# A two-layer diffusion backbone: the later modulation vectors formed by VectorE alone

## The chip, the cores and the metric

The kernel runs on one NeuronCore of a Trainium2 chip. The metric is the device time of one execution in microseconds (us), the median of several runs. The engines are named as the profile names them: PE is TensorE (matmuls; PEld is its weight load), DVE is VectorE, ACT is ScalarE, POOL is GpSimd, SP is the engine whose queue issues the DMAs.

## The reference, cut to what matters

Two layers (`DEPTH = 2`) work on 256 latent tokens and 256 context tokens of width 1024. Each layer is a half feed-forward, a token mixer of four branches, and another half feed-forward. Each of these three is modulated by shift, scale and gate vectors that come from one large product per layer:

```python
for l in range(DEPTH):
    mod_x = jax.nn.silu(c) @ w_mod[l] + b_mod[l]        # 1024 -> 9 * 1024
    mod_c = (jax.nn.silu(c_ctx) @ w_mod[l] + b_mod[l])[None, :]
    ...
    x, xc = layer(x, xc, mod_x, mod_c, p, ctx_out)

def half_ffn(t, m, i):
    j = 6 * i
    hh = adaln(t, g[2 * i], m[j], m[j + 1])             # rms_norm(t, g) * (1 + scale) + shift
    return t + 0.5 * m[j + 2] * swiglu(hh, p['ffn_w_gate'][i], p['ffn_w_up'][i], p['ffn_w_down'][i])
```

So `w_mod` (two layers of 1024 x 9216) is multiplied by only two vectors, SiLU(c_ctx) and SiLU(c). Everything is float32.

## The kernel before, in words

Activations lie with features on partitions, `x[0..7]`, each 128 x 512 (256 context columns, then 256 latent ones). A weight tile of up to 128 x 2048 comes by one DMA into one of three `w` buffers. ACT copies it to a rounded high part `wh` (L150) and DVE subtracts to get the low part `wl` (L151), in halves; there are four buffers each of `wh` and `wl`, that is two tiles. `mm3` (L191 to L193) forms every product out of three matmuls: high by high, high by low, low by high. `ffn` runs, for each half of the hidden width, eleven gate-and-up tiles (`gu`: 2 x 8 products, 48 matmuls into the PSUM tiles A and B; `act` then multiplies on DVE at L455 and splits at L196 and L197) and eight down tiles (`dn`: 11 products, 33 matmuls, and the residual at L422). `plan` writes the order of the weight stream.

The 9216 modulation columns of a layer are 18 sets `s` of four blocks of 128. The first four sets of layer 0 are made at the start on PE (`mod_set`). The other 32 are made in the background of feed-forwards: `plan` puts 64 `mod` tiles (32 sets, two halves `h` of the input width) between the `gu` and `dn` tiles, 28 of them in the first feed-forward of layer 0, 12 in its second, 24 in the first of layer 1. `mod_bg` handles a tile. The tile has 128 input features on partitions and four blocks `k` of 512 modulation columns; for each block and for each of the two vectors `v`, DVE multiplies the block with the vector's 128 values (a scalar for each partition) and adds it to a running sum, L254 for the first and L256 for the others, 8 instructions a tile. This leaves two 128 x 512 partial sums in `ya` buffers. When two sets are ready, eight matmuls with a one-hot column matrix `sel` (L265, into PSUM D) add the 128 partitions up. After one or two such pairs ACT copies D out (L269), four transposes (L272, into C) put the features on partitions, and L277 adds the bias. `derive` makes the scale and gate constants of it.

The order on each engine is settled when the program is built, by a list scheduler that works from its own costs and from free buffers. Each engine then runs its row of instructions strictly in that order, waiting where a row's inputs or buffers aren't ready. The neighbourhood branch's bias tables are fetched (`nr`, small strided DMAs) and masked (`nb`) by `na_bias`, both pairs of heads at once at the branch's start.

Of the kernel before, what the change touches and what calls it, by code (L numbers as in the profile page):

```python
# [15 lines left out]
L = 2  # L16
D = 1024
# [12 lines left out]
O_G, O_BM, O_BG, O_CA, O_LW, O_LB, O_BA, O_BX, O_LAM = 0, 24, 96, 128, 134, 142, 144, 148, 152  # L30
# [5 lines left out]
class Net:  # L36
# [16 lines left out]
    BUFS = dict(b=12, nb=4, nr=4, ya=4, yp=4, m=8, a=6, l=5, r=3, t=2)  # L53
# [52 lines left out]
    def start_stream(self):  # L106
        self.q = self.plan()
        self.raw, self.split = {}, {}
        self.at_raw = self.at_split = self.at = 0
        tags = ["b"] * 12 + ["ya"] * 4 + ["yp"] * 4 + ["a"] * 4 + ["b"] * 8  # L110
        self.first = {}
        for s in range(4):
            if s == 1:
                self.fetch()
                self.fetch()
            for k in range(KC):
                t = self.blk(tags.pop(0))
                self.nc.sync.dma_start(t, self.a["mod"][0, s, k // 4][:, 512 * (k % 4):512 * (k % 4) + 512])
                self.first[s, k] = t
# [79 lines left out]
    def consts(self):  # L199
        nc = self.nc  # L200
# [9 lines left out]
        self.sv = self.sc[:, :, 0:2]  # L210
        self.sel = self.cp.tile([128, 2, 32], F32, name="sel")
# [14 lines left out]
        for c in range(KC):  # L226
# [3 lines left out]
                     (self.rep[0], self.a["rep"][0]), (self.rep[1], self.a["rep"][1])]  # L230
        self.part, self.group = {}, {}
# [12 lines left out]
    def mod_bg(self, l, s, h):  # L244
        nc = self.nc
        w = self.take("mod", l, s, h)[:].rearrange("p (k n) -> p k n", k=4)
        if h == 0:
            self.part[s] = [self.blk("ya"), self.blk("ya")]
        for k in range(4):
            for v in range(2):  # L250
                acc = self.part[s][v]
                sv = self.sv[:, 4 * h + k, v:v + 1]
                if h == 0 and k == 0:
                    nc.vector.tensor_scalar(acc, w[:, k], sv, None, op0=ALU.mult)  # L254
                else:
                    nc.vector.scalar_tensor_tensor(acc, w[:, k], sv, acc, op0=ALU.mult, op1=ALU.add)  # L256
        r = s % 6
        if h == 1 and r % 2 == 1:
            j = (r % 4) // 2
            last = r in (3, 5)  # L260
            if r in (1, 5):
                self.group = self.ps("D")
            g = self.group
            for q in range(4):
                nc.tensor.matmul(g[32 * q:32 * q + 32, :], self.sel[:, j], self.part[s - 1 + q // 2][q % 2],  # L265
                                 start=(r in (1, 5)), stop=last, tile_position=(0, 32 * q))
            if last:
                sb = self.blk("t")
                nc.scalar.activation(sb, g, AF.Copy)  # L269
                pt = self.ps("C", (128, 4, 128))  # L270
                for b in range(4):
                    nc.tensor.transpose(pt[:, b], sb[:, 128 * b:128 * b + 128], self.ident)  # L272
                v = pt[:].rearrange("p b (g v n) -> p g b v n", g=2, v=2)
                for jj in range(2 if r == 3 else 1):
                    s0 = s - 3 + 2 * jj if r == 3 else s - 1
                    bm = self.par[l][:, O_BM + 4 * s0:O_BM + 4 * s0 + 8].rearrange("p (g b) -> p g b", g=2)
                    nc.vector.tensor_tensor(self.mods[l][:, s0:s0 + 2], v[:, :, :, :, jj],  # L277
                                            bm.unsqueeze(3).to_broadcast([128, 2, 4, 2]), op=ALU.add)
                    self.derive(l, s0)
                    self.derive(l, s0 + 1)  # L280
# [276 lines left out]
    def na_bias(self, l, pr):  # L557
        nc = self.nc
        src = self.a["nb"]
        nb = []  # L560
        for h in (2 * pr, 2 * pr + 1):
            raw = self.blk("nr", (128, 2, 4, 64))
            for qb in range(2):
                for r in range(2):
                    o = src.offset + (l * 4 + h) * 465 + (7 - (2 * qb + r)) * 31 - 48
                    ap = bass.AP(tensor=src.tensor, offset=o, ap=[[1, 64], [31, 4], [1, 64]])
                    nc.sync.dma_start(raw[64 * r:64 * r + 64, qb], ap)
            t = self.blk("nb", (128, 2, 4, 64))
# [100 lines left out]
    def attend(self, step, segs, out, keys, queries, value, biases, sink):  # L669
# [7 lines left out]
        def scores(u):  # L677
# [8 lines left out]
            P[u] = self.softmax(S, nk(u), (lambda hh: bias[pr](hh, qb)) if sg else None, lambda hh: sink(pr, hh))  # L686

# [15 lines left out]
        for pr in range(2):  # L703
            bias[pr] = biases(pr)
# [59 lines left out]
    def mixer(self, l, H, nxt):  # L764
# [160 lines left out]
    def run(self):  # L925
# [45 lines left out]
def layout(x, c, ctx, c_ctx, w_mod, b_mod, norm_g, ffn_w_gate, ffn_w_up, ffn_w_down, w_in, b_gate, conv_a_w,  # L971
# [13 lines left out]
    A["mod"] = wm.transpose(0, 4, 1, 3, 2, 5, 6).reshape(L, 18, 2, 128, 2048)  # L985
# [57 lines left out]
```

## Time and profile before

| | us |
|---|---|
| median of 3 runs (2058.46 to 2063.48) | 2061.11 |
| the profiled execution's own time | 2066.55 |
| its span, first to last instruction | 2064.8 |
| PE busy | 2037.9 (99%) |
| DVE busy | 1311.4 (64%) |
| ACT busy | 805.3 (39%) |

Busy is the time in which an engine has at least one instruction in work. Two instructions in a row overlap: one starts before the record of the one ahead has ended. What an engine can do in a stretch is therefore read from start to start, and not from the mean length of one record.

### The profile page before, as it was taken

How to read it: one execution, taken by the hardware profiler on the slowest of the kernel's cores; microseconds unless marked ns; L12 is line 12 of the kernel's file. 1: busy time of each engine (PE TensorE's matmuls, PEld its weight loads, DVE VectorE, ACT ScalarE, POOL GpSimd, SP SyncE). 2: the span in 40 equal slices, each digit the busy share in tenths (PEclk: the TensorE clock that was granted, in tenths of full speed). 3: DMA queues.
4: the chain of work that ended last, by engine and by line, in shares of the span. 5: the costliest groups of instructions: out<-in, count | busy, mean ns of one | idle time of the engine just before them, and what ended most of it. 6: DMA issues, size and time to landing. Idle time of an engine off the chain costs nothing.

```text
span 2064.8 us, 29629 instructions
## 1 busy us (share of the span) xinstructions
PE 2037.9 (99%) x11937; PEld 1740.5 (84%) x11937; DVE 1311.4 (64%) x2357; ACT 805.3 (39%) x1321; POOL 87.8 (4%) x90
## 2 busy tenths in 40 slices
PE   7999999999999999999999999999999999999999
PEld 4877888897797788888888888878888999999999
DVE  4877877577546545677633357677754777775554
ACT  3322232356434434232222233222323676664443
POOL 0000000210010000100000010000002101000000
PEclk9999999999999999999999999999999999999999
DMA  9654555521222234144432234445533224463453
GB/s 336 176 178 166 204 184 179 173 75 52 72 95 77 66 101 156 62 164 180 156 123 78 82 133 148 170 166 204 184 131 124 82 90 143 141 231 136 173 196 119
DMA packets 61402, 294.45 MB, mean 143 GB/s; under 512 B 14672, under 2 KB 16336, under 8 KB 38224
## 3 DMA queue, kind: packets, MB, share of 16 engines
q1 hardware_dynamic: 61264, 292.55, 41.1%
q8 instruction: 94, 1.54, 0.3%
q14 instruction: 44, 0.36, 0.1%
HBM read 291.48 MB, written 1.05 MB: 142 GB/s over the span
## 4 chain that ended last, share of the span: by engine, by line
PE 94%; DMA 2%; DVE 2%; ACT 1%; issue 1%; POOL 0%; SPq 0%; POOLq 0%; ACTq 0%; DVEq 0%
PE A L191 19%; PE A L192 18%; PE A L193 18%; PE B L191 11%; PE B L192 11%; PE B L193 11%; PE B L684 1%; DMA b<-in_mod 1%; PE D L696 1%; DMA w<-in_gu 1%; PE C L664 1%; PE D L265 1%; DVE ya L256 1%; PE E L734 1%; DVE wl L151 0%
## 5 line engine op out<-in xcount | busy, mean ns | idle before, releaser
L150 ACT ACTIVATE wh<-w 128x1024 fp32r<-128x1024 f32 (+2 forms) x476 | 429.6, 906 | 881.4 <-PE A L192 403.0
L151 DVE TENSOR_TENSOR wl<-w,wh 128x1024 fp32r<-128x1024 f32 (+2 forms) x476 | 489.9, 1031 | 320.8 <-ACT wh L150 316.6
L191 PE MATMUL A<-h,wh 128*128 128x512 f32 (+1 forms) x1440 | 509.3, 354 | 6.2 <-ACT wh L150 3.8
L193 PE MATMUL A<-h,wl 128*128 128x512 f32 (+1 forms) x1440 | 497.9, 346 | 0.0
L192 PE MATMUL A<-h,wh 128*128 128x512 f32 (+1 forms) x1440 | 497.3, 345 | 0.0
L191 PEld LDWEIGHTS A<-h,wh 128*128 128x128 f32 x1440 | 273.7, 190 | 58.4 <-ACT wh L150 13.5
L256 DVE SCALAR_TENSOR_TENSOR ya<-w,sc,ya 128x512 f32<-128x512 f32 x448 | 309.5, 745 | 10.9 <-DMA w<-in_mod 9.9
L193 PEld LDWEIGHTS A<-h,wl 128*128 128x128 f32 x1440 | 274.1, 190 | 34.3 <-DVE wl L151 1.7
L192 PEld LDWEIGHTS A<-h,wh 128*128 128x128 f32 x1440 | 274.1, 190 | 30.9 <-issue 0.6
L191 PE MATMUL B<-h,wh 128*128 128x512 f32 (+1 forms) x736 | 262.2, 357 | 0.0
L192 PE MATMUL B<-h,wh 128*128 128x512 f32 (+1 forms) x736 | 261.8, 356 | 0.0
L193 PE MATMUL B<-h,wl 128*128 128x512 f32 (+1 forms) x736 | 261.8, 356 | 0.0
L191 PEld LDWEIGHTS B<-h,wh 128*128 128x128 f32 x736 | 139.8, 190 | 20.0 <-ACT wh L150 0.4
L192 PEld LDWEIGHTS B<-h,wh 128*128 128x128 f32 x736 | 139.9, 190 | 19.7 <-issue 0.4
L193 PEld LDWEIGHTS B<-h,wl 128*128 128x128 f32 x736 | 139.7, 190 | 19.5
L455 DVE TENSOR_TENSOR t<-t,B 128x512 f32<-128x512 f32 (+1 forms) x88 | 54.2, 618 | 116.6 <-PE B L193 115.6
L330 POOL TENSOR_TENSOR nb<-nb,l 128x256 f32<-128x256 f32 x45 | 47.6, 1074 | 1344.6 <-ACT l L328 1344.6
L191 PE MATMUL A<-b,wh 128*128 128x512 f32 (+1 forms) x246 | 85.1, 346 | 0.0
L193 PE MATMUL A<-b,wl 128*128 128x512 f32 (+1 forms) x246 | 85.0, 345 | 0.0
L192 PE MATMUL A<-b,wh 128*128 128x512 f32 (+1 forms) x246 | 84.9, 345 | 0.0
L191 PE MATMUL B<-b,wh 128*128 128x512 f32 (+1 forms) x204 | 73.5, 360 | 0.0
L192 PE MATMUL B<-b,wh 128*128 128x512 f32 (+1 forms) x204 | 73.4, 360 | 0.0
(271 smaller groups left out, 2941.1 us busy)
## 6 DMA issues: line engine op xcount, KB each, us to landing
w<-in_gu SPq DMA_DIRECT2D x88, 1024.0 KB, 4.8
w<-in_mod SPq DMA_DIRECT2D x64, 1024.0 KB, 4.8
w<-in_dn SPq DMA_DIRECT2D x64, 704.0 KB, 4.1
w<-in_gb SPq DMA_DIRECT2D x64, 640.0 KB, 3.9
w<-in_fm SPq DMA_DIRECT2D x10, 1024.0 KB, 4.8
w<-in_tm SPq DMA_DIRECT2D x10, 1024.0 KB, 4.9
w<-in_wo SPq DMA_DIRECT2D x8, 1024.0 KB, 4.8
b<-in_mod SPq DMA_DIRECT2D x20, 256.0 KB, 5.7
```

The lines of the kernel that those rows point to most:

```text
L150: nc.scalar.activation(hi[i][:, :e], t[:, o:o + e], AF.Copy)
L151: nc.vector.tensor_tensor(lo[i][:, :e], t[:, o:o + e], hi[i][:, :e].bitcast(F32), op=ALU.subtract)
L191: mm(ps, wh, xh, start=first, stop=False)
L192: mm(ps, wh, xl, start=False, stop=False)
L193: mm(ps, wl, xh, start=False, stop=last)
L256: nc.vector.scalar_tensor_tensor(acc, w[:, k], sv, acc, op0=ALU.mult, op1=ALU.add)
L265: nc.tensor.matmul(g[32 * q:32 * q + 32, :], self.sel[:, j], self.part[s - 1 + q // 2][q % 2], start=(r in (1, 5)), stop=last, tile_positi ...
L330: nc.gpsimd.tensor_tensor(n["acc"][s], n["acc"][s], sq, op=ALU.add)
L455: nc.vector.tensor_tensor(s[:, lo:hi], s[:, lo:hi], ps[1][:, lo:hi], op=ALU.mult)
L664: nc.tensor.transpose(pt[:, j], p[:, 128 * j:128 * j + 128], self.ident)
L684: nc.tensor.matmul(S[hh][:, 256 * j:256 * j + 256], queries(sg, j)[rows, pr, qw], keys(j, pr)[rows], start=True, stop=True)
L696: nc.tensor.matmul(y[64 * hh:64 * hh + 64, 128 * qb:128 * qb + 128], value(j, pr, hh), T[u, hh][:, j], start=(j == 0), stop=(j == n - 1), ...
```

## The change

The 64 `mod` tiles of the background are laid out the other way: modulation features on partitions, the 1024 input features along the row (two blocks `g` of two chunks `k` of 512 for each tile). The two vectors are brought in as a tile `rows` that holds the same 2 x 1024 values on all 128 partitions (one more DMA of 1 MB behind the other late constants, and one SiLU over 2048 columns on ACT). For each block, vector and chunk DVE runs one `tensor_tensor_reduce`, a multiply and a sum along 512 columns into a single value for each partition. The element-wise product goes to a scratch tile `junk`, one of the six `a` buffers, that nobody reads. When the set's second half is done, two small additions join the chunks and add the bias. The matmuls with `sel`, the copy and the transposes are gone. The first four sets are made as before from an array of their own. With this the `nb` and `nr` buffers go from four to two each, and the neighbourhood branch's tables are fetched and masked for one pair of heads at a time, the second pair in the middle of the branch.

```diff
-    BUFS = dict(b=12, nb=4, nr=4, ya=4, yp=4, m=8, a=6, l=5, r=3, t=2)
+    BUFS = dict(b=12, nb=2, nr=2, ya=4, yp=4, m=8, a=6, l=5, r=3, t=2)
...
+        self.rows = self.cp.tile([128, 2, 2, 512], F32, name="rows")
...
-                     (self.rep[0], self.a["rep"][0]), (self.rep[1], self.a["rep"][1])]
+                     (self.rep[0], self.a["rep"][0]), (self.rep[1], self.a["rep"][1]), (self.rows, self.a["rows"])]
...
     def mod_bg(self, l, s, h):
-        w = self.take("mod", l, s, h)[:].rearrange("p (k n) -> p k n", k=4)
+        w = self.take("mod", l, s, h)[:].rearrange("p (g k n) -> p g k n", g=2, k=2)
         if h == 0:
-            self.part[s] = [self.blk("ya"), self.blk("ya")]
-        for k in range(4):
+            self.part = self.small((128, 4, 2, 2), "mr", 3)
+        junk = self.blk("a")
+        for g in range(2):
             for v in range(2):
-                acc = self.part[s][v]
-                sv = self.sv[:, 4 * h + k, v:v + 1]
-                if h == 0 and k == 0:
-                    nc.vector.tensor_scalar(acc, w[:, k], sv, None, op0=ALU.mult)
-                else:
-                    nc.vector.scalar_tensor_tensor(acc, w[:, k], sv, acc, op0=ALU.mult, op1=ALU.add)
-        r = s % 6
-        if h == 1 and r % 2 == 1:
...
-            for q in range(4):
-                nc.tensor.matmul(g[32 * q:32 * q + 32, :], self.sel[:, j], self.part[s - 1 + q // 2][q % 2],
-                                 start=(r in (1, 5)), stop=last, tile_position=(0, 32 * q))
-            if last:
-                sb = self.blk("t")
-                nc.scalar.activation(sb, g, AF.Copy)
-                pt = self.ps("C", (128, 4, 128))
-                for b in range(4):
-                    nc.tensor.transpose(pt[:, b], sb[:, 128 * b:128 * b + 128], self.ident)
...
+                for k in range(2):
+                    nc.vector.tensor_tensor_reduce(out=junk, in0=w[:, g, k], in1=self.rows[:, v, k], scale=1.0, scalar=0.0,
+                                                   op0=ALU.mult, op1=ALU.add,
+                                                   accum_out=self.part[:, 2 * h + g, v, k:k + 1])
+        if h == 1:
+            m = self.mods[l][:, s]
+            bm = self.par[l][:, O_BM + 4 * s:O_BM + 4 * s + 4]
+            nc.vector.tensor_tensor(m, self.part[:, :, :, 0], self.part[:, :, :, 1], op=ALU.add)
+            nc.vector.tensor_tensor(m, m, bm.unsqueeze(2).to_broadcast([128, 4, 2]), op=ALU.add)
+            self.derive(l, s)
...
+            if pr == 0 and u == U[len(U) // 2 - 1]:
+                bias[1] = biases(1)
...
+        nc.scalar.activation(self.rows, self.rows, AF.Silu)
```

**PE, first feed-forward, where the first pair of sets is ready.** Before, the matmuls with `sel` (L265) stand between two `gu` tiles and the transposes (L272) between two matmuls of the next tile:

```order
L193 MATMUL B_913<-h_202,wl_895 128x512
L265 MATMUL D_987<-ya_744,sel 32x512
L265 MATMUL D_987<-ya_745,sel 32x512
L265 MATMUL D_987<-ya_900,sel 32x512
L265 MATMUL D_987<-ya_901,sel 32x512
L191 MATMUL A_1004<-h_188,wh_971 128x512
L192 MATMUL A_1004<-h_189,wh_971 128x512
L193 MATMUL A_1004<-h_188,wl_973 128x512
L191 MATMUL A_1004<-h_190,wh_971 128x512
L192 MATMUL A_1004<-h_191,wh_971 128x512
L272 MATMUL C_994<-cst,t_992 128x128 x4
```

In the changed kernel the same place reads:

```order
L193 MATMUL B_916<-h_199,wl_898 128x512
L191 MATMUL A_996<-h_185,wh_974 128x512
L192 MATMUL A_996<-h_186,wh_974 128x512
L193 MATMUL A_996<-h_185,wl_976 128x512
L191 MATMUL A_996<-h_187,wh_974 128x512
L192 MATMUL A_996<-h_188,wh_974 128x512
L193 MATMUL A_996<-h_187,wl_976 128x512
```

The `gu` matmuls now follow each other with nothing between them.

**DVE, the same feed-forward, some tiles later.** Before, one tile's instructions alternate between two running sums, so that each waits for the one before the last:

```order
L256 SCALAR_TENSOR_TENSOR ya_1071<-w_1002,sc,ya_1071 128x512 [waits DMAHW1_49,DVE_49]
L256 SCALAR_TENSOR_TENSOR ya_1072<-w_1002,sc,ya_1072 128x512 [waits DVE_49]
L151 TENSOR_TENSOR wl_1144<-w_1061,wh_1142 128x1024 [waits DMAHW6_49,PE_49,Activation_49]
L256 SCALAR_TENSOR_TENSOR ya_1071<-w_1002,sc,ya_1071 128x512 [waits DVE_49]
L256 SCALAR_TENSOR_TENSOR ya_1072<-w_1002,sc,ya_1072 128x512 [waits DVE_49]
```

In the changed kernel (line numbers of its own: L249 is the multiply-and-sum, L432 the old L455) each is a pair of instructions, the main one and the read of the accumulator, and each main one of a tile writes the same scratch tile `a`, so that it waits for the pair ahead of it:

```order
L249 ISA a_1064,mr_1063<-w_913,rows 128x512 [waits DVE_49]
L249 ISA mr_1063 128x1
L249 ISA a_1064,mr_1063<-w_913,rows 128x512 [waits DVE_49]
L249 ISA mr_1063 128x1
L249 ISA a_1064,mr_1063<-w_913,rows 128x512 [waits DVE_49]
L249 ISA mr_1063 128x1
L151 TENSOR_TENSOR wl_1057<-w_972,wh_1055 128x1024 [waits DMAHW5_49,PE_49,Activation_49]
L432 TENSOR_TENSOR t_965<-t_965,B_916 128x512 [waits PE_49]
L151 TENSOR_TENSOR wl_1058<-w_972,wh_1056 128x1024 [waits Activation_49]
L197 TENSOR_TENSOR b_969<-t_965,b_968 128x512 [waits Activation_49]
```

The number of large instructions for each tile stays at eight; the wait at the head of each is now for the one just ahead.

**ACT, at the end of the first norm.** Before, the last four activations of the normed input (`h`, L375) stand together, with the first split of the next weight tile behind them:

```order
L375 ACTIVATE h_200<-l_609,mods_81 128x256 [waits DVE_49]
L375 ACTIVATE h_200<-l_613,mods_81 128x256 [waits DVE_49]
L375 ACTIVATE h_202<-l_617,mods_81 128x256 [waits DVE_49]
L375 ACTIVATE h_202<-l_621,mods_81 128x256 [waits DVE_49]
L150 ACTIVATE wh_333<-w_311 128x1024 [waits DMAHW1_49,PE_49]
```

Now (L352 is the old L375) the SiLU of `rows` stands ahead of the last of them:

```order
L352 ACTIVATE h_197<-l_608,mods_81 128x256 [waits DVE_49]
L352 ACTIVATE h_197<-l_612,mods_81 128x256 [waits DVE_49]
L352 ACTIVATE h_199<-l_616,mods_81 128x256 [waits DVE_49]
L921 ACTIVATE rows<-rows 128x2048 [waits DMAHW1_49]
L352 ACTIVATE h_199<-l_620,mods_81 128x256 [waits DVE_49]
L150 ACTIVATE wh_332<-w_310 128x1024 [waits DMAHW2_49,PE_49]
```

So one activation that PE waits for has moved behind a long one.

## Rows read from the trace of the kernel before

**Rows 1.** The page, part 1: busy us, share of the span, instructions.

```profile
PE 2037.9 (99%) x11937; PEld 1740.5 (84%) x11937; DVE 1311.4 (64%) x2357; ACT 805.3 (39%) x1321; POOL 87.8 (4%) x90
```

**Rows 2.** Lines L265 and L272 on PE: count, ns min/median/max, first and last start.

```profile
L265 PE MATMUL D<-ya,sel x128: 592/605/617, 103.4 to 1529.0; 128*32 128x512 f32 x128
...
L272 PE MATMUL C<-cst,t x44: 270/272/477, 110.2 to 1531.1; 128*128 128x128 f32 x44
```

**Rows 3.** Chain that ended last, 240 to 345 us: start us, us, what.

```profile
250.89 1.00 PE D L265 x8
...
296.12 0.99 PE D L265 x8
...
340.87 1.00 PE D L265 x8
```

**Rows 4.** PE in order of time: start us, us, instruction.

```profile
234.41 0.39 PE L191 MATMUL B<-h,wh 128*128 128x512 f32 x1
...
239.85 0.39 PE L191 MATMUL A<-h,wh 128*128 128x512 f32 x1
```

**Rows 5.** Around 96 to 116 us: PE's waits, the chain, busy time by window.

```profile
PE C L272 <- ACT t L269: 4.4, 1, 4.4
...
96.39 9.62 DMA w<-in_gu
...
110.22 1.12 PE C L272 x4
111.34 0.43 PE A L193
...
110.00:120.00 10.00, 9.78 (x36) 8.04 (x37) 7.17 (x15) 0.77 (x2) 0.00 (x0) 0.75 0.80 186
```

**Rows 6.** DVE by line and shape: count | busy us, mean ns | idle before.

```profile
L256 DVE SCALAR_TENSOR_TENSOR ya<-w,sc,ya 128x512 f32<-128x512 f32 x448 | 309.5, 745 | 10.9 <-DMA w<-in_mod 9.9
L151 DVE TENSOR_TENSOR wl<-w,wh 128x1024 fp32r<-128x1024 f32 x228 | 278.9, 1225 | 171.2 <-ACT wh L150 167.4
...
L455 DVE TENSOR_TENSOR t<-t,B 128x512 f32<-128x512 f32 x66 | 44.9, 684 | 99.7 <-PE B L193 99.2 <-ACT t L454 0.5
...
L640 DVE CUSTOM_DVE_ANT_0 B<-B,nb 128x256 f32<-128x256 f32 x16 | 6.5, 445 | 1.6 <-PE B L684 1.4
...
L743 DVE SCALAR_TENSOR_TENSOR r<-r,b 128x512 f32<-128x512 f32 x8 | 5.5, 690 | 4.0 <-ACT r L735 4.0
...
L755 DVE TENSOR_TENSOR_SCAN ya<-r,r 128x512 f32<-128x512 f32 x4 | 4.9, 1220 | 0.1
...
L640 DVE DVE_READ_ACCUMULATOR2_ANT mx<- 128x1 f32 x32 | 4.5, 142 | 0.0
```

**Rows 7.** DVE in order of time at three places: start us, us, instruction.

```profile
55.63 0.17 DVE L519 TENSOR_SCALAR lr<-lr 128x4 f32<-128x4 f32 x1
55.83 0.16 DVE L521 TENSOR_TENSOR lr<-lr,lr 128x4 f32<-128x4 f32 x1
...
230.04 1.23 DVE L151 TENSOR_TENSOR wl<-w,wh 128x1024 fp32r<-128x1024 f32 x1
231.18 4.72 DVE L256 SCALAR_TENSOR_TENSOR ya<-w,sc,ya 128x512 f32<-128x512 f32 x7
...
489.84 0.43 DVE L640 CUSTOM_DVE_ANT_0 B<-B,nb 128x256 f32<-128x256 f32 x1 [0.56 <-PE B L684]
...
490.19 0.46 DVE L640 CUSTOM_DVE_ANT_0 B<-B,nb 128x256 f32<-128x256 f32 x1
```

**Rows 8.** ACT in order of time, 234 us; in brackets idle time and what ended it.

```profile
234.38 1.06 ACT L150 ACTIVATE wh<-w 128x1024 fp32r<-128x1024 f32 x1 [4.38 <-PE A L192]
```

**Rows 9.** ACT in order of time, 55 to 59 us, and the DMA table: KB, us to landing.

```profile
55.56 0.51 ACT L375 ACTIVATE h<-l,mods 128x256 fp32r<-128x256 f32 x1 [1.05 <-DVE l L374]
57.29 2.01 ACT L150 ACTIVATE wh<-w 128x1024 fp32r<-128x1024 f32 x2 [1.23 <-PE A L192]
...
w<-in_gu SPq DMA_DIRECT2D x88, 1024.0 KB, 4.8
```

More of the change, by code (lines that the diff above doesn't have):

```diff
@@ L117, in start_stream @@
                 t = self.blk(tags.pop(0))
-                self.nc.sync.dma_start(t, self.a["mod"][0, s, k // 4][:, 512 * (k % 4):512 * (k % 4) + 512])
+                self.nc.sync.dma_start(t, self.a["first"][s, k // 4][:, 512 * (k % 4):512 * (k % 4) + 512])
                 self.first[s, k] = t
@@ L217, in consts @@
         nc.vector.memset(self.ones, 1.0)
-        nc.vector.memset(self.sel, 0.0)
-        for j in range(2):
-            nc.vector.memset(self.sel[:, j, j:j + 1], 1.0)
         nc.vector.memset(self.mhalf, -0.5)
@@ L257, in mod_bg @@
-        r = s % 6
-        if h == 1 and r % 2 == 1:
[L259 to L263, printed above, removed]
-            for q in range(4):
-                nc.tensor.matmul(g[32 * q:32 * q + 32, :], self.sel[:, j], self.part[s - 1 + q // 2][q % 2],
-                                 start=(r in (1, 5)), stop=last, tile_position=(0, 32 * q))
-            if last:
-                sb = self.blk("t")
-                nc.scalar.activation(sb, g, AF.Copy)
-                pt = self.ps("C", (128, 4, 128))
-                for b in range(4):
-                    nc.tensor.transpose(pt[:, b], sb[:, 128 * b:128 * b + 128], self.ident)
[L273 to L280, printed above, removed]
@@ L567, in na_bias, with na_mask @@
                     nc.sync.dma_start(raw[64 * r:64 * r + 64, qb], ap)
+            raws.append(raw)
+        return raws
+    def na_mask(self, raws):
+        nc = self.nc
+        nb = []
+        for raw in raws:
             t = self.blk("nb", (128, 2, 4, 64))
@@ L701, in values @@
                 nc.scalar.activation(out[pr][:, 256 * sg:256 * sg + 256], y, AF.Copy)
-        for pr in range(2):
-            bias[pr] = biases(pr)
+        bias[0] = biases(0)
         while self.pending:
@@ L984, in layout @@
     wm = w_mod.reshape(L, 2, 4, 128, 72, 128)[:, :, :, :, sets]
-    A["mod"] = wm.transpose(0, 4, 1, 3, 2, 5, 6).reshape(L, 18, 2, 128, 2048)
+    A["first"] = wm[0, :, :, :, :4].transpose(3, 0, 2, 1, 4, 5).reshape(4, 2, 128, 2048)
+    A["mod"] = w_mod.reshape(L, D, 72, 128)[:, :, sets].transpose(0, 2, 3, 4, 1).reshape(L, 18, 2, 2, 128, D) \
+        .transpose(0, 1, 2, 4, 3, 5).reshape(L, 18, 2, 128, 2048)
+    A["rows"] = np.broadcast_to(np.stack([c_ctx, c[0]]).reshape(1, 2, 2, 512), (128, 2, 2, 512))
     gu = np.stack([ffn_w_gate, ffn_w_up], axis=2).reshape(L, 2, 2, KC, 128, FT, 128)
```

12 lines of the change are left out of this document (6 added, 6 removed).

## The prediction, made before the changed kernel was run

> **What bounds the kernel now.** I read the page's busy times first. PE is busy for 2037.9 of 2064.8 us and DVE for 1311.4 [rows 1], so a microsecond of PE work that goes is a microsecond of time, wherever DVE and the DMAs keep up behind it. The second view was PE's two lines that the change deletes [rows 2], the third the chain around them [rows 3], where they stand between the ordinary matmuls and nothing runs beside them. The fourth was DVE, in its order of time [rows 7]: it has room on average, but it carries all 64 `mod` tiles inside three feed-forwards, and there I made its budget for one `gu` tile.
>
> **What PE is rid of.** An ordinary matmul of 512 columns costs PE 0.2267 us from start to start: 24 of them lie between 234.41 and 239.85 [rows 4]. A `gu` tile of 48 is 10.88 us. L265 has 128 matmuls in 16 groups of eight, L272 has 44 in eleven groups of four [rows 2]. The record of one L265 matmul (605 ns) is no price, since four run side by side and the next tile's first matmul starts late. The price is the extra time of a stretch that holds them. From 296.12 to 340.87 there are four tiles (43.53) and one group of eight: 44.75, so a group costs 1.22. From 250.89 to 296.12 the stretch holds a group of transposes as well: 45.23, so four transposes cost 0.48 [rows 3]. Sum: 16 x 1.22 = 19.5, and ten groups at 0.48 with the first one at 1.12 [rows 5] = 5.9. Together 25.4 us.
>
> The first transposes cost more than their work. PE waited 4.4 us in front of the first four for ACT's copy L269 [rows 5]. That copy stood behind ACT's split of a `gu` tile whose DMA took 9.62 us. The wait was not for PE's own next matmuls: the order puts L272 in the middle of a tile that PE had already begun. Without it PE goes on. [...] Both go: 6.4 us. In all PE loses 31.8 us.
>
> **What DVE gets in exchange.** Before, eight L256 start 0.66 apart (seven in 4.72 us, the last 0.745 long [rows 6, 7]), 5.3 us a tile. A `wl` of 1024 columns takes 1.14 from start to start [rows 7], about 0.08 less than its record; at the same 0.08 less, L455 and L197 take 0.60 each (684 ns [rows 6]). A `gu` tile with a `mod` tile beside it is 2 x 1.14 + 1.2 + 5.3 = 8.8 us of DVE against 10.88 of PE.
>
> The multiply-and-sum of 512 columns out of SBUF isn't in this trace. Its nearest row is L640, the same kind of instruction (add and maximum) over 256 columns with one input in PSUM: 445 ns, its accumulator read 142 ns [rows 6], and 0.35 us from one such pair to the next [rows 7]. L455's 684 ns for 512 columns with one input in PSUM and L743's 690 with both in SBUF [rows 6] say that the place of the inputs hardly matters. 512 columns more cost a subtraction 1225 - 684 = 541 ns [rows 6], so 256 more are 0.27, and the pair comes to 0.62 from start to start. That is the lower bound, with the read hidden as at 489.84. But here each main instruction waits for the pair ahead, for the scratch tile's sake. In a chain where each waits for the last, the next starts 0.03 after the record's end (L519 to L521, 0.20 apart and 0.17 long [rows 7]). With the read and this step the pair costs 0.62 + 0.14 + 0.03 = 0.80, rounded up; this value I take. The upper bound is the slowest two-input row of 512 columns: the scan L755 with 1.22 [rows 6], plus the same 0.17: 1.39.
>
> At 0.80 a tile costs 6.4 us and, with the small additions (two and `derive`, some 0.2 for each tile), the `gu` budget is 3.5 + 6.4 + 0.2 = 10.1 of 10.88. It fits, with 7% left. In the `dn` tiles five of eight carry a `mod` tile, and by the same count (two `wl` of 768 and 640 columns and two residuals of 256, by the same 1.06 ns a column about 2.4, an estimate) a half needs 8 x 2.4 + 5 x 6.6 = 52 of 8 x 33 x 0.2267 = 59.8. A delay has room too: ACT can split a tile when PE has read half of the tile two before it [rows 8], and DVE's `wl` of it is ready by 237, while PE, which began a tile at 228.97 (24 matmuls before 234.41), needs it two tiles later at 250.7. So DVE can be 14 us late before PE stands still.
>
> If the pair takes p, DVE's work in the three stretches (20, 9 and 19 `gu` tiles at 3.7 without the pairs, and the 24 `dn` tiles between the first and the last `mod` tile at 2.4) comes to 234 + 512p us, against 48 x 10.88 + 24 x 7.48 = 701 of PE and 3 x 14 of slack: the first microsecond is lost at p = 1.0 (0.95 in the longest stretch), and the whole gain at about 1.05.
>
> [...]
>
> **The rest.** The SiLU of 2048 columns stands ahead of the last activation of `h`. ACT is free there from 54.51 and takes about 1.9 us for 2048 columns, by the two splits of 1024 in 2.01, so that activation starts near 56.4 in place of 55.56 [rows 9]: 0.9 lost if PE needs it at once, nothing if not; I take 0.9. The 1 MB of `rows` comes ahead of the third `gu` tile and delays it by at most 4.8 us; the split of that tile waits for PE and not for its DMA [rows 9], so this is free. Between 60 and 110 us the weight buffers are held by `mod` tiles until DVE has read them, and one DMA was late already (9.62). DVE's longer tiles delay such DMAs by 1 to 3 us; only eight instead of sixteen of the small `nr` DMAs stand between them, which helps. I take 1 us for this, with bounds of -1 and 6. The later masking of the second pair of heads moves the same instructions to a place where DVE has room; its fetches stand ahead of `gb` weights on SP, 0 to 3 us, I take 1.
>
> The sum: 2066.55 - 31.8 + 0.9 + 1 + 1 = 2037.7 for an execution like the profiled one. That one lies 5.4 us above the median of the runs, so the median should come to about 2033. Without a stall and with all small terms at their better end it is 2028.
>
> **The rivals.**
> *DVE becomes the bound (slower).* Place: the `gu` tiles of the three stretches. At p = 1.39 DVE needs 234 + 712 = 946 against 743, which is 203 lost: about 2235 us. It decides from p = 1.05 on. For it: the scan's 1.22, and an instruction that multiplies and adds in one pass. [...] Chance 0.11.
> *DVE comes just to the edge.* p between 0.95 and 1.05, or the fixed order of DVE's row, made for other costs, keeps PE waiting now and then. Half the gain gone: 2040 to 2058, say 2048. For it: 7% of room is little, and in the first 50 us DVE is ahead of PE by only 1 to 2 us. Against it: the 14 us. Chance 0.15.
> *PE's start stays starved.* The stall at 105 us isn't that of the transposes but of the 9.62 us DMA, and comes back in front of the next `gu` matmuls: 6.4 less gained, 2039. Chance 0.12.
> *No change.* The deleted work would have to lie beside other PE work; [rows 3] speak against it. With this goes a stall in the mixer that eats the gain. 2061, chance 0.04.
>
> **How the numbers follow.** The forecast (2026 to 2038) has 0.53; below that 0.05. From 2022 to 2058 are the forecast and its better end, the starved start and DVE at the edge, 0.85 in all; this is the range. A change of 0.2% (4 us) is about what the runs can tell from none. Faster by more: 0.53 + 0.05 + 0.12 + 0.14 = 0.84. Within it: 0.04 and a little of the edge, 0.05. Slower: 0.11.
>
> **What would show it.** PE's busy time falls by about 26 us and its wait in front of the transposes is gone. The multiply-and-sum has a record of 0.70 to 0.72 us, with pairs 0.75 to 0.82 apart; a record of 1.2 us or more makes the prediction wrong, and then `wl` L151 becomes what PE's L193 waits for. DVE in the window from 230 to 290 us is about 90% busy. ACT's SiLU ends near 56.4. If PE has waits of several us for `wl` or `wh` between 60 and 120 us, the start is what I have mis-sized.

## The result and the profile after

| | before | after |
|---|---|---|
| median of 4 runs, us | 2062.3 (2058.46 to 2063.64) | 2040.16 (2039.99 to 2041.47) |
| profiled execution, us | 2066.55 | 2040.34 |

The ratio is 0.9899, with a 95% interval of 0.9887 to 0.9911: 1.0% faster. Predicted were 2033 us and a range of 2022 to 2058; the point lies 7 us too low. The page of the changed kernel, part 1, to be read beside [rows 1]:

```profile
PE 2010.8 (99%) x11765; PEld 1732.7 (85%) x11765; DVE 1331.3 (65%) x2914; ACT 800.3 (39%) x1311; POOL 87.3 (4%) x90
```

PE is still the bound: it lost 172 matmuls (128 and 44, [rows 2]) and 27 us of busy time. The new instruction (L249, where [rows 6] have L256), count, ns min/median/max, first and last start:

```profile
L249 DVE CUSTOM_DVE_ANT_0 a<-w,rows x512: 671/691/1232, 62.6 to 1488.0; 128x512 f32<-128x512 f32 x171
L249 DVE DVE_READ_ACCUMULATOR2_ANT mr<- x512: 72/82/89, 63.2 to 1488.6; 128x1 f32 x171
```

DVE in order of time, where each pair waits for the one ahead:

```profile
93.98 0.69 DVE L249 CUSTOM_DVE_ANT_0 a<-w,rows 128x512 f32<-128x512 f32 x1
94.60 0.08 DVE L249 DVE_READ_ACCUMULATOR2_ANT mr<- 128x1 f32 x1
94.72 0.70 DVE L249 CUSTOM_DVE_ANT_0 a<-w,rows 128x512 f32<-128x512 f32 x1
```

A pair that waits comes 0.74 after the last. Where the pairs of two tiles alternate, with a scratch tile each, they come 0.61 apart. DVE in the window from 230 to 290 us, between the steady `gu` tiles (busy us of PE, PEld, DVE, ACT, POOL; PEclk; DMA share; GB/s):

```profile
230.00:290.00 60.00, 60.00 (x267) 49.69 (x266) 53.42 (x130) 18.20 (x23) 0.00 (x0) 1.00 0.53 197
```

DVE is busy for 53.4 of 60 us and PE for all 60. PE's waits after the start-up, from 40 to 900 us (us in total, times, longest):

```profile
PE D L318 <- ACT l L305: 1.7, 1, 1.7
PE A L193 <- DVE wl L151: 1.6, 3, 0.8
PE A L191 <- ACT wh L150: 1.0, 1, 1.0
PE E L337 <- POOL r L333: 0.7, 2, 0.4
PE A L192 <- DVE h L353: 0.7, 1, 0.7
PE E L585 <- DVE m L593: 0.6, 1, 0.6
PE B L191 <- ACT wh L150: 0.4, 1, 0.4
PE B L193 <- DVE wl L151: 0.3, 1, 0.3
```

The 4.4 us in front of the transposes [rows 5] are gone. In their place there are small ones for L318, L193, L191 and L192, which the kernel before did not have. Where they lie is read from stages. Each number below is the time between two starts of ACT's SiLU of a gate tile (L454 before, L431 after), worked out from the traces; the 88 of them are numbered from 0 in order of time. Tiles 2 to 10 are the first half of the first feed-forward, 10 to 21 its first `dn` tiles and its second half, 21 to 22 its last `dn` tiles and mixer 0, 22 to 43 the second feed-forward up to its last `gu` tile, 43 to 65 the third, 65 to 87 its `dn` tiles, mixer 1 and the fourth:

```
us              2 to 10   10 to 21   21 to 22   22 to 43   43 to 65   65 to 87       sum
before        97.31      185.78     534.58     276.47     376.66     491.02    1961.82
tables_only   90.53      185.77     534.45     276.49     376.69     491.01    1954.93
after         87.61      179.86     538.77     271.53     367.09     490.78    1935.63
tables_no_pe  87.66      179.47     532.75     271.53     367.19     492.06    1930.66
moved         87.61      179.52     532.79     271.55     367.07     492.05    1930.58
```

The last two rows and the second are experiments, below; the sum is the time from tile 2 to tile 87. The changed kernel gains in every stage with `mod` tiles, except in the third column. There it needs 4.2 us more than before, although one group of matmuls and transposes is gone there too.

DVE in that stage, in order of time:

```profile
354.24 2.22 DVE L151 TENSOR_TENSOR wl<-w,wh 128x768 fp32r<-128x768 f32 x2
356.38 1.22 DVE L249 CUSTOM_DVE_ANT_0 a<-w,rows 128x512 f32<-128x512 f32 x1
357.87 0.68 DVE L249 CUSTOM_DVE_ANT_0 a<-w,rows 128x512 f32<-128x512 f32 x1
```

GpSimd and PE beside it (in brackets idle time and what ended it):

```profile
354.65 2.40 POOL L307 TENSOR_TENSOR nb<-nb,l 128x256 f32<-128x256 f32 x2 [306.50 <-ACT l L305]
...
353.69 0.50 PE L191 MATMUL A<-b,wh 128*128 128x512 f32 x1 [0.99 <-ACT wh L150]
355.24 0.50 PE L193 MATMUL A<-b,wl 128*128 128x512 f32 x1 [0.81 <-DVE wl L151]
```

The window from 338 to 363 us:

```profile
338.00:363.00 25.00, 22.82 (x99) 17.96 (x97) 24.43 (x71) 4.84 (x10) 2.40 (x2) 1.00 0.48 147
```

From 338 to 363 us DVE works for 24.4 of 25 us: pairs of the last `gu` tile's `mod` tile and of those of the `dn` tiles 0, 1 and 2 stand one behind the other. The `wl` that PE needs comes behind them, and while GpSimd adds (L307), DVE's own instructions take up to 1.22 us in place of 0.68. PE waits 2.7 us in five places between 353 and 372 us. Half of that is for `wh`, and there the path goes over the three weight buffers: a buffer is free for the next weight tile only when DVE is through with the tile in it. The DMA queue's longest wait from 335 to 370 us, and a piece of the chain that ended last:

```profile
SPq L128 <- DVE mr L249: 12.3, 3, 9.0
```

```profile
361.04 9.05 DMA w<-in_dn
```

The `dn` tile that ACT splits at 352.80 was issued at 348.70, right behind a tile's last pair at 347.99; the one of the second line landed 9 us after its issue. The second place is near 830 us, at the end of mixer 0; DVE, then PE:

```profile
830.74 1.23 DVE L249 CUSTOM_DVE_ANT_0 a<-w,rows 128x512 f32<-128x512 f32 x1
832.01 1.08 DVE L249 CUSTOM_DVE_ANT_0 a<-w,rows 128x512 f32<-128x512 f32 x1
833.03 0.47 DVE L399 SCALAR_TENSOR_TENSOR x<-A,G,x 128x256 f32<-128x256 f32 x1
...
834.07 0.30 PE L318 MATMUL D<-l,ones 128*32 128x128 f32 x1 [1.71 <-ACT l L305]
```

Pairs of the next feed-forward's `mod` tiles stand in DVE's row ahead of a residual (L399); ACT squares its result (L305), and that square is what PE waits for.

### The profile page after: what moved, and what is told of

It is laid out like the page before. It is cut to its first block, busy times and chain, and to the rows that moved or that the text cites. A ratio compares the mean times of both kernels' runs of the same rounds, so it can differ in the third digit from the quotient of the medians.

```text
span 2038.6 us, 29838 instructions
## 1 busy us (share of the span) xinstructions
PE 2010.8 (99%) x11765; PEld 1732.7 (85%) x11765; DVE 1331.3 (65%) x2914; ACT 800.3 (39%) x1311; POOL 87.3 (4%) x90
## 3 DMA queue, kind: packets, MB, share of 16 engines
HBM read 292.53 MB, written 1.05 MB: 144 GB/s over the span
## 4 chain that ended last, share of the span: by engine, by line
PE 93%; DVE 3%; issue 2%; DMA 1%; ACT 1%; POOL 0%; SPq 0%; POOLq 0%; ACTq 0%; DVEq 0%
PE A L191 19%; PE A L192 18%; PE A L193 18%; PE B L191 11%; PE B L192 11%; PE B L193 11%; DVE a L249 1%; PE B L668 1%; PE D L682 1%; PE C L648 1%; PE E L719 1%; DVE wl L151 1%; DMA w<-in_dn 0%; ACT wh L150 0%; PE D L265 0%
## 5 line engine op out<-in xcount | busy, mean ns | idle before, releaser
L191 PE MATMUL A<-h,wh 128*128 128x512 f32 (+1 forms) x1440 | 506.9, 352 | 5.8 <-ACT wh L150 3.3
L193 PE MATMUL A<-h,wl 128*128 128x512 f32 (+1 forms) x1440 | 496.2, 345 | 1.2 <-DVE wl L151 1.1
L192 PE MATMUL A<-h,wh 128*128 128x512 f32 (+1 forms) x1440 | 496.3, 345 | 0.7 <-DVE h L353 0.7
L249 DVE CUSTOM_DVE_ANT_0 a<-w,rows 128x512 f32<-128x512 f32 x512 | 350.4, 695 | 41.1 <-DMA w<-in_mod 32.3
L191 PEld LDWEIGHTS A<-h,wh 128*128 128x128 f32 x1440 | 273.2, 190 | 48.3 <-issue 11.5
L193 PEld LDWEIGHTS A<-h,wl 128*128 128x128 f32 x1440 | 273.4, 190 | 35.1 <-DVE wl L151 2.5
L192 PEld LDWEIGHTS A<-h,wh 128*128 128x128 f32 x1440 | 273.5, 190 | 31.8 <-DVE h L353 1.4
L191 PE MATMUL B<-h,wh 128*128 128x512 f32 (+1 forms) x736 | 262.2, 356 | 0.0
L193 PE MATMUL B<-h,wl 128*128 128x512 f32 (+1 forms) x736 | 261.7, 356 | 0.0
L192 PE MATMUL B<-h,wh 128*128 128x512 f32 (+1 forms) x736 | 261.7, 356 | 0.0
L191 PEld LDWEIGHTS B<-h,wh 128*128 128x128 f32 x736 | 139.8, 190 | 19.9 <-ACT wh L150 0.4
L192 PEld LDWEIGHTS B<-h,wh 128*128 128x128 f32 x736 | 139.7, 190 | 19.6 <-issue 0.4
L193 PEld LDWEIGHTS B<-h,wl 128*128 128x128 f32 x736 | 139.6, 190 | 19.6
L432 DVE TENSOR_TENSOR t<-t,B 128x512 f32<-128x512 f32 (+1 forms) x88 | 54.2, 619 | 107.4 <-PE B L193 106.4
L307 POOL TENSOR_TENSOR nb<-nb,l 128x256 f32<-128x256 f32 x45 | 47.2, 1066 | 1320.0 <-ACT l L305 1320.0
L191 PE MATMUL A<-b,wh 128*128 128x512 f32 (+1 forms) x246 | 85.4, 347 | 1.0 <-ACT wh L150 1.0
L193 PE MATMUL A<-b,wl 128*128 128x512 f32 (+1 forms) x246 | 85.1, 346 | 1.1 <-DVE wl L151 1.1
L192 PE MATMUL A<-b,wh 128*128 128x512 f32 (+1 forms) x246 | 84.9, 345 | 0.0
L191 PE MATMUL B<-b,wh 128*128 128x512 f32 (+1 forms) x204 | 73.1, 358 | 0.4 <-ACT wh L150 0.4
L193 PE MATMUL B<-b,wl 128*128 128x512 f32 (+1 forms) x204 | 73.1, 358 | 0.3 <-DVE wl L151 0.3
```

The lines of the kernel that those rows point to most:

```text
L191: mm(ps, wh, xh, start=first, stop=False)
L192: mm(ps, wh, xl, start=False, stop=False)
L193: mm(ps, wl, xh, start=False, stop=last)
L249: nc.vector.tensor_tensor_reduce(out=junk, in0=w[:, g, k], in1=self.rows[:, v, k], scale=1.0, scalar=0.0, op0=ALU.mult, op1=ALU.add, accum ...
L307: nc.gpsimd.tensor_tensor(n["acc"][s], n["acc"][s], sq, op=ALU.add)
L432: nc.vector.tensor_tensor(s[:, lo:hi], s[:, lo:hi], ps[1][:, lo:hi], op=ALU.mult)
```

## The experiments

**1. Parts of the change alone.** The first leaves the PE work out of the kernel before, the second makes only the tables' part, the third makes both.

```diff
 # no_pe_work, and tables_no_pe on top of tables_only
-            for q in range(4):
-                nc.tensor.matmul(g[32 * q:32 * q + 32, :], self.sel[:, j], self.part[s - 1 + q // 2][q % 2],
...
             if last:
-                nc.scalar.activation(sb, g, AF.Copy)
...
-                    nc.tensor.transpose(pt[:, b], sb[:, 128 * b:128 * b + 128], self.ident)
-                v = pt[:].rearrange("p b (g v n) -> p g b v n", g=2, v=2)
+                v = self.part[s][0][:, 0:32].rearrange("p (b g v n) -> p g b v n", b=4, g=2, v=2)
 # tables_only
-    BUFS = dict(b=12, nb=4, nr=4, ya=4, yp=4, m=8, a=6, l=5, r=3, t=2)
+    BUFS = dict(b=12, nb=2, nr=2, ya=4, yp=4, m=8, a=6, l=5, r=3, t=2)
...
+    def na_fetch(self, l, pr):
...
+                bias[1] = biases(1)
```

no_pe_work:

> The kernel before without the matmuls with the one-hot matrix, the copy and the transposes; DVE's 512 multiply-and-adds stay, and the bias is added to a piece of a partial sum, so the later modulation values are not the reference's. The prediction's PE term (25.4 us of PE work and 6.4 us of the wait with its clock): 31.8 us less than before, a ratio of 0.9846. Rival, the wait near 105 us belongs to the late DMA and comes back before the next gate-and-up matmuls: 25.4 us less, ratio 0.9877. If the 6.6 us that the changed kernel loses again near 350 and 830 us come from its own DVE instructions, none of them is here; if they come from the shorter PE work alone, they are here too and the ratio is near 0.988.

Measured: 2041.52 us, ratio 0.9897 (0.9882 to 0.9912). That is 21.5 us less than before in the same series (2063.0), short of both numbers. But from 60 to 160 us PE doesn't wait, and the clock is full, although a `gu` tile is late here too (issued at 96.24 us, split by ACT at 104.42). The window, then ACT:

```profile
60.00:160.00 100.00, 100.00 (x443) 82.83 (x442) 80.71 (x122) 28.59 (x40) 0.00 (x0) 1.00 0.61 194
...
104.42 1.06 ACT L150 ACTIVATE wh<-w 128x1024 fp32r<-128x1024 f32 x1 [2.89 <-DMA w<-in_gu]
```

So the wait did not come back before other matmuls, and that rival's mechanism falls, by the trace and not by the time. As a price of the PE work this run is no use: it has new waits of its own, which no other run shows (1.05, 1.26 and 1.21 us at 166, 348 and 393 us, for the split of the activation and for GpSimd's sum). They don't make up the whole shortfall; the rest wasn't traced.

tables_only:

> The kernel before with only the new treatment of the neighbourhood tables (two buffers, one pair of heads at a time). The prediction took 1 us more, with bounds 0 and 3: ratio 1.0005. From the landmarks of the two traces, which show no loss inside either mixer: 0, ratio 1.000. Rival, the fetches in the middle of the branch hold weights up: 3 us or more, ratio 1.0015.

Measured: 2059.72 us (12 runs, 2057.93 to 2061.22), ratio 0.9986 (0.9977 to 0.9994). It is faster, which none of the three numbers had. By the stages nothing changes in the mixers (534.45 against 534.58, 491.01 against 491.02), but 6.8 us go in the first one: the transposes are still there, and PE does not wait for them. The DMA issue, ACT, and the window at the same place:

```profile
95.60 0.33 SPq L128 DMA_DIRECT2D w<-in_gu  x1
...
100.68 1.06 ACT L150 ACTIVATE wh<-w 128x1024 fp32r<-128x1024 f32 x1 [2.71 <-DMA w<-in_gu]
...
100.00:110.00 10.00, 10.00 (x50) 7.35 (x50) 7.76 (x14) 3.68 (x5) 0.00 (x0) 1.00 0.52 201
```

The tables' small DMAs are half as many here before 110 us. The `gu` tile that took 9.62 us before [rows 5] is issued at 95.60, and ACT begins its split at 100.68, 5.1 us later. The wait of the kernel before needed both: the copy that had to stand behind the split, and the late tile. Either edit alone takes it away: here the tile is early, in no_pe_work it is late and there is no copy behind it.

tables_no_pe:

> The kernel before with the new treatment of the neighbourhood tables and without the matmuls with the one-hot matrix, the copy and the transposes; DVE keeps its multiply-and-adds, and the bias is added to a piece of a partial sum, so the later modulation values are not the reference's. This is the change without its new DVE work. PE is rid of 25.4 us by the prediction's count, against 2059.7 us with the tables alone: 2034.3, ratio to before 0.986. Then the changed kernel's 2040.2 has 6 us that its DVE instructions cost. Rival, the deleted PE work was worth less, 18 to 20 us: 2040 us, ratio 0.989, and the new DVE work costs nothing.

Measured: 2033.01 us, ratio 0.9854 (0.9839 to 0.9868), near the 2034.3 that was expected; the rival of 2040 falls. By the stages the PE work is worth 1954.93 - 1930.66 = 24.3 us. And the changed kernel needs 1935.63 - 1930.66 = 5.0 us more than its own change without the new DVE work: 6.0 in the third column, and -1.3 in the last, which wasn't traced.

By the medians it needs 7.2 us more (2040.16 against 2033.01). The rest lies ahead of the table: ACT begins tile 2's gate SiLU at 63.3 us in this execution and at 65.8 in that of the changed kernel. The SiLU of `rows`, which this run doesn't have either, makes PE wait 0.7 of these 2.5 us. The remainder isn't explained; the start differs as much (65.8 and 67.6) between the changed kernel and the probe of section 3, which is the same kernel up to its end.

**2. The kernel before again,** for further profiled executions.

> The kernel before once more, for a second profiled execution. The one shown first took 2066.55 us and had PE wait 4.4 us in front of the first transposes near 110 us, with the clock at half behind it. Theory: this wait is not in every execution; it is most of the spread of the runs (2059 to 2067 us), so an execution near 2060 us has none, and the prediction took the 6.4 us off twice, once as the wait and once as the distance of the profiled execution from the median. Rival: the wait is there in every execution, also in one near 2060, and the spread has another place.

Measured: one execution of 2068.01 us, with the wait.

> The kernel before a third time. Two profiled executions of it, of 2066.6 and 2068.0 us, both had the wait of 4 us in front of the first transposes; its timed runs went from 2059 to 2067. Theory: an execution of 2062 us or less has no such wait and no half clock near 110 us, one of 2064 or more has both. Rival: the wait is there at every time of the run, and the runs differ elsewhere.

Measured: one execution of 2066.49 us, with the wait. PE's waits from 60 to 200 us in the two:

```profile
PE C L272 <- ACT t L269: 4.0, 1, 4.0
```

```profile
PE C L272 <- ACT t L269: 4.6, 1, 4.6
```

Both lie at the upper end of a kernel whose timed runs go from 2059 to 2068 us, or above it. The theory's other half stays open: no execution near 2060 us was profiled. Two things on record lean to it. The edit that removes 6.8 us from the trace removes 2063.0 - 2059.7 = 3.3 us from the median. And with 37 timed runs of this kernel the mean granted clock is recorded: it is 0.997 or 0.998 in all 14 of up to 2062.4 us and 0.994 to 0.996 in all 14 from 2064.8 us on, while the three profiled executions with the wait have 0.994 or 0.995. A mean doesn't tell where in a run the clock fell.

**3. The pair by itself.** Series of one kind behind all other work of the changed kernel:

```diff
+        series(0, src[0], r0, [one])          # one scratch tile
+        series(12, src[1], r0, [one, two])    # two in turn
+        series(24, bank, r0, [one, two])      # bank: a PSUM tile
+        for i in range(12):
+            nc.gpsimd.tensor_tensor(pool[i % 2][:, 0:256], src[2][:, 0:256], r0[:, 0:256], op=ALU.add)
+        series(36, src[2], r0, [one])
+        series(48, big[:, 0:1024], wide, [big[:, 1024:2048]], 8)
```

> The changed kernel with series of the multiply-and-sum behind all its work, for their own price. One scratch tile, each waiting for the pair ahead: 0.735 us apart. Two scratch tiles in turn: 0.61. One source in PSUM, two scratch tiles: 0.61 if the place of the sources hardly matters; if two SBUF sources halve the rate, then the row with one source in PSUM is the fast one, about half of the others. One scratch tile beside GpSimd's additions of 256 columns out of SBUF: 1.15 to 1.2 where the two meet, if it is they that make the long records of 1.1 to 1.23 us; 0.735 if not. 1024 columns, one scratch: 0.735 + 0.54 = 1.27.

Two rows of each series, DVE in order of time:

```profile
2039.98 0.69 DVE L938 CUSTOM_DVE_ANT_0 a<-m,rows 128x512 f32<-128x512 f32 x1
2040.72 0.69 DVE L938 CUSTOM_DVE_ANT_0 a<-m,rows 128x512 f32<-128x512 f32 x1
...
2049.13 0.69 DVE L938 CUSTOM_DVE_ANT_0 a<-m,rows 128x512 f32<-128x512 f32 x1
2049.74 0.69 DVE L938 CUSTOM_DVE_ANT_0 a<-m,rows 128x512 f32<-128x512 f32 x1
...
2057.34 0.69 DVE L938 CUSTOM_DVE_ANT_0 a<-C,rows 128x512 f32<-128x512 f32 x1
2057.95 0.69 DVE L938 CUSTOM_DVE_ANT_0 a<-C,rows 128x512 f32<-128x512 f32 x1
...
2066.77 1.08 DVE L938 CUSTOM_DVE_ANT_0 a<-m,rows 128x512 f32<-128x512 f32 x1
2067.90 1.09 DVE L938 CUSTOM_DVE_ANT_0 a<-m,rows 128x512 f32<-128x512 f32 x1
...
2081.23 1.23 DVE L938 CUSTOM_DVE_ANT_0 w<-w,rows 128x1024 f32<-128x1024 f32 x1
2082.49 1.23 DVE L938 CUSTOM_DVE_ANT_0 w<-w,rows 128x1024 f32<-128x1024 f32 x1
```

From start to start: 0.74 with one scratch tile, 0.61 with two, 0.61 with a source in PSUM, 1.13 beside GpSimd, 1.26 for 1024 columns. With two scratch tiles it makes no difference whether one source lies in PSUM. Of what was tried, GpSimd's additions slow the instruction down most.

**4. More of the pairs.** Four or all eight of a tile are done twice.

```diff
+                    if k == 0:                         # twelve; without this line sixteen
+                        nc.vector.tensor_tensor_reduce(out=junk, in0=w[:, g, k], in1=self.rows[:, v, k], scale=1.0, scalar=0.0,
...
```

> The changed kernel with 12 multiply-and-sums for each modulation tile in place of 8 (four are done twice). At the measured 0.61 to 0.735 us, say 0.66, a tile's pairs take 7.9 us, which stands for p = 0.99 in the prediction's formula: DVE 234 + 512 x 0.99 = 741 us against 743. The prediction's edge: the first microsecond is lost here, so 0 to 10 us more than the changed kernel, 2040 to 2050. Rival, DVE has little room already, since losses near 350 us are its own: 15 us more or beyond, over 2055.

Measured: 2066.54 us, ratio 1.0013 (1.0003 to 1.0023), 26 us above the changed kernel; the rival is right. Of these 26, 14 lie in the third column (552.67 against 538.77), 6 in the second. PE's waits from 345 to 400 us:

```profile
PE B L191 <- ACT wh L150: 4.4, 1, 4.4
PE B L193 <- DVE wl L151: 3.6, 2, 2.9
PE A L191 <- ACT wh L150: 1.8, 1, 1.8
PE A L193 <- DVE wl L151: 0.8, 1, 0.8
```

> The changed kernel with each multiply-and-sum done twice, 16 for each tile: 10.6 us of pairs, as p = 1.32 in the prediction's formula, DVE 234 + 676 = 910 us against 743, that is 167 us lost: 2040 + 167 = 2207 us, if DVE becomes the bound as the prediction's first rival says. If instead DVE's row leaves PE more slack than the formula has, less; over 2230 if the waits for weight buffers that DVE holds add to it.

Measured: 2198.88 us, ratio 1.0653 (1.0630 to 1.0676). The formula is 8 us off at a loss of 159. Far beyond the edge it holds. At the edge it fails, since it is one sum and lets a slow place borrow from all others; the run with twelve shows the loss at such a place.

**5. Scratch tiles and places.**

```diff
-        junk = self.blk("a")                                   # two_scratch
+        junk = [self.blk("a"), self.blk("a")]                  # out=junk[k]
-    SLOTS = (1, 2, 4, 5, 7), (0, 1, 2)                         # spread
+    SLOTS = (1, 2, 4, 5, 7), (1, 3, 5)
+    FIRST = {(0, 0): 2, (0, 1): 5, (1, 0): 3, (1, 1): 2}
...
-                if bg and half * FH + m >= 2:
+                if bg and half * FH + m >= self.FIRST[l, i]:
```

> The changed kernel with two scratch tiles used in turn, so that no multiply-and-sum waits for the pair just ahead. Every pair should then start 0.61 us after the last, in place of 0.61 to 0.735. Theory: the losses near 350 and 830 us come from the place of the pairs in DVE's row, and there they stood 0.61 apart already; so the time changes by less than 1 us, ratio to before 0.989 to 0.990. Rival, the length of the pair sets the losses: 3 us or more less, ratio below 0.9885.

Measured: 2038.88 us, ratio 0.9885 (0.9870 to 0.9900); the intervals overlap. In the trace the third column falls by 3.4 us (535.36) and the waits near 350 us are gone; the one near 830 us stays (2.0). So at the first place the rival has it, but its cause isn't told apart from another: with the second scratch tile the scheduler also puts the low part of a `dn` tile further ahead in DVE's row, ahead of pairs that it follows in the changed kernel (there at 354.24):

```profile
350.47 0.95 DVE L151 TENSOR_TENSOR wl<-w,wh 128x768 fp32r<-128x768 f32 x1
```

> The changed kernel with its modulation tiles at other places of the weight stream: in the second half of the first feed-forward behind the down tiles 1, 3 and 5 in place of 0, 1 and 2; in layer 0's second feed-forward from gate-and-up tile 5 on in place of 2, in layer 1's first from 3 on. Theory: the 3.8 us lost near 350 us and the 2.2 us near 830 and 870 us come from DVE's row, where pairs stand bunched ahead of residuals and low parts that PE needs; they go, 5 to 6 us less than the changed kernel, ratio to before 0.9865 to 0.9875. Rival, the late weight DMA of 9 us near 361 sets the first of them: then 2 us less at most, ratio 0.989.

Measured: 2041.69 us, ratio 0.9897 (0.9883 to 0.9912), no gain. The wait near 830 us is gone, but the first place got a larger one. PE, and DVE's waits from 355 to 396 us:

```profile
395.15 0.74 PE L319 MATMUL D<-nb,ones 128*32 128x128 f32 x3 [5.30 <-POOL nb L308]
```

```profile
DVE a L250 <- DMA w<-in_mod: 6.6, 1, 6.6
DVE wl L152 <- ACT wh L151: 3.0, 1, 3.0
```

and ACT behind the second of these waits:

```profile
390.28 2.00 ACT L151 ACTIVATE wh<-w 128x1024 fp32r<-128x1024 f32 x2 [4.50 <-DMA w<-in_fm]
```

A `mod` tile that is fetched later lands later (issued at 365.35, landed at 375.04). DVE waits for it, so its pairs end later, and with them a weight buffer comes free later: the mixer's first tile (`fm`) is issued at 384.51 and lands at 390.18. ACT's split of it is late, DVE waits for that split with residuals queued behind, and the sum of squares behind those is late for PE.

**6. No `mod` tile between the last `dn` tiles.** Four tiles (the gate sets 16 and 17 of layer 0) go into the second feed-forward, which begins its own at `gu` tile 5.

```diff
-            return [(0, s, h) for s in range(4, 18) for h in range(2)]
+            return [(0, s, h) for s in range(4, 16) for h in range(2)]
...
-            return [(1, s, h) for s in range(6) for h in range(2)]
+            return [(0, s, h) for s in (16, 17) for h in range(2)] + [(1, s, h) for s in range(6) for h in range(2)]
...
-                if bg and half * FH + m >= 2:
+                if bg and half * FH + m >= self.FIRST[l, i]:     # 5 for (0, 1), else 2
```

> The changed kernel with four of its modulation tiles (the gate sets 16 and 17 of layer 0) taken from the first feed-forward into the second, where they begin at gate-and-up tile 5; so no modulation tile stands between the last down tiles of the first feed-forward. Theory: the losses near 350 us (2.7 us of PE's waits, 3.8 by the landmarks) come from tiles that stand one behind the other between down tiles of 7.5 us, and the 1.7 us near 834 from pairs ahead of a residual; both go, 4 to 5.5 us less than the changed kernel, 2035 to 2036, ratio to before 0.9865 to 0.9875. Rival, as when the tiles were spread: a late weight DMA takes the place of the wait, 2039 to 2042, ratio 0.989 or more.

Measured: 2035.46 us, ratio 0.9862 (0.9846 to 0.9879). PE's waits from 60 to 900 us:

```profile
PE E L338 <- POOL r L334: 0.7, 2, 0.4
PE E L586 <- DVE m L594: 0.6, 1, 0.6
PE A L194 <- DVE wl L152: 0.5, 1, 0.5
```

By the stages it is as fast as the change without its DVE work (1930.58 and 1930.66); its median is 2.5 us above that run's, and its tile 2 comes 2.8 us later (66.1 and 63.3). Both places lie in the third column, and both waits are gone.

> The same with two scratch tiles used in turn. If the length of the pair matters only where tiles stand one behind the other, nothing is left for it to gain: within 1 us of the kernel with the moved tiles alone. If pairs of 0.735 us cost something elsewhere, 1 us or more less.

Measured: 2035.10 us, ratio 0.9861 (0.9846 to 0.9876): nothing is left to gain there. These two are the best versions of the study, 1.4% faster than before.

## Why the prediction was right, and where its number was off

The measured 2040.16 us lies above the band of the main forecast (2026 to 2038). It is inside the range because the range takes in two rivals, and one of them is what happened in part: DVE at the edge, put at 2040 to 2058. The other, a start that stays starved, has the nearest number (2039), but that is chance: PE doesn't wait for a weight tile there.

**PE's work: right.** Predicted 25.4 us, measured 24.3 (tables_only to tables_no_pe). A group with its transposes was put at 1.70, and 1.70 is what goes in the third column (534.45 to 532.75), which has one.

**The wait with its clock: right in the trace, counted twice in the sum.** The prediction put 6.4 us on it, the first column gives 6.8. Of the 6.4, 4.4 are the wait [rows 5]. No run shows the other 2 us as such: in the trace of the kernel before, the nine matmuls from 111.34 us [rows 5] to 115.13 take 3.8 us, where 9 x 0.2267 are 2.0, so 1.8 us more, at a granted clock of 0.50 in each microsecond from 110 to 114. The end of that piece of the chain:

```profile
114.33 0.43 PE A L191
114.76 0.38 PE A L192
115.13 0.23 PE A L193
```

The prediction's reading that the wait was the transposes' own also holds (no_pe_work). It named the late tile too, but took the fewer table fetches for a help only, and so gave the tables' part of the change a loss of 1 where it is a gain of 3.3 by itself. The step that failed is the last one: 5.4 us were taken off because the profiled execution lies above the median, as if all later terms held for the median too. But three profiled executions of the kernel before (2066.55, 2068.01, 2066.49) have the wait, and its removal is worth 3.3 us in the median. The changed kernel's profiled execution lies at its median (2040.34 and 2040.16). So the sum for the execution, 2037.7, was the better forecast, though in part by luck: it lacks DVE's 5 us, and 2 us that it put elsewhere did not come. How often the wait comes in the timed runs is open.

**The pair: mis-sized, without harm.** Predicted 0.80, measured 0.61 to 0.74. The accumulator's read takes 82 ns, not the 142 of L640 [rows 6], and a pair that waits starts 0.05 us behind the record of the main instruction ahead (93.98 + 0.69, then 94.72): the read lies within that, where the prediction set it on top of the 0.62. The lower bound of 0.62, from two rows of different widths, was right.

**The place of the sources: right.** That it hardly matters was read from L455 and L743 [rows 6]. The probe has 0.61 us from pair to pair with both sources in SBUF and 0.61 with one in PSUM.

**The `gu` budget: right.** DVE was to be 90% busy from 230 to 290 us; it is 89%, and PE doesn't wait.

**The `dn` tiles: the step that failed.** The prediction counted a half with five `mod` tiles on eight `dn` tiles (52 of 59.8 us), and one sum over whole stretches with 14 us of slack. The second half of the first feed-forward has its three `mod` tiles on the first three `dn` tiles, straight behind the `gu` tiles. A `dn` tile lasts 33 x 0.2267 = 7.5 us for PE; DVE needs 2.4 (the prediction's estimate) + 8 x 0.61 to 0.74 = 7.3 to 8.3 there, and more beside GpSimd's sums of squares (up to 1.22 us for a multiply-and-sum, at 356.38), which only this half has. The tiles stand so close that DVE also frees the weight buffers late, a delay that the prediction had put at 1 us, and at the start. With the pairs ahead of a residual near 830 us DVE's new work cost 5.0 us in all by the stages, where the prediction had put 2.9 us on other places. That is its rival of DVE at the edge, at p = 0.61 to 0.74 and not at 0.95. That the places were the cause is shown: with four tiles moved, the loss is gone (moved). How the 6.0 us divide between late `wl`, late weight tiles and GpSimd isn't shown.

**The small terms.** SiLU: 0.9 predicted. It takes 1.90 us, as forecast, and ends at 55.2 and not 56.4; PE waits 0.7 us for `h` (L353) in the changed kernel, and not in those without the SiLU. The start's 1 and the mixer's 1 are not there (87.61 against 87.66; 534.45 against 534.58).

**The corrected sum:** 2059.7 (tables alone, median) - 24.3 + 5.0 = 2040.4, against 2040.16. This shows that the stages hold the whole difference between tables_only and the changed kernel. How it divides into 24.3 and 5.0 rests on one execution of tables_no_pe; by the medians it is 26.7 and 7.2.

## What to carry to other kernels

Make the budget of an engine that fills gaps tile by tile, at the tightest one, and not over a stretch: an engine with 35% of its time free still cost 5 us, where its background work stood three times in a row on the shortest tiles and ahead of a residual. Count as well when it frees the buffers that the next fetch waits for. Don't take a wait off a profiled time and then also the distance of that time from the median, since the wait may be that distance. Before work in the background is made faster, see whether it can stand elsewhere: other places for a few tiles gave 4.7 us, pairs that don't wait for each other nothing on top.

## What the runs showed of the hardware

Two kinds of DVE instruction with both sources in SBUF are slower beside GpSimd's additions out of SBUF: the multiply-and-sum comes 1.13 us from pair to pair in place of 0.74 (the probe), and two `wl` of 768 columns take 2.22 us (at 354.24, in the changed kernel) in place of 1.69 (at 362.89). What makes them slower isn't shown. At one place of the kernel before, a residual with one source in PSUM lies wholly inside such an addition and takes 0.48 us, the median of its line being 478 ns. GpSimd, then DVE:

```profile
1851.32 1.14 POOL L330 TENSOR_TENSOR nb<-nb,l 128x256 f32<-128x256 f32 x1 [2.67 <-ACT l L328]
...
1851.98 0.48 DVE L422 SCALAR_TENSOR_TENSOR x<-B,G,x 128x256 f32<-128x256 f32 x1
```

A multiply-and-sum of 1024 columns, each waiting for the one ahead (1.26), is about as dear as two of 512 on two scratch tiles (1.22) and cheaper than two on one (1.47). So a longer row and a second scratch tile save about the same.
